# Token rows of a recurrent mixer: 128x128 transposes of two chunks and 64-partition evacuations in place of pairs of 64x64 products

## The chip, the cores and the metric

The kernel runs on one core of one Trainium2 chip. The time is the device time of one execution in microseconds (us). The core has TensorE (PE in the profile; its weight loads are PEld), VectorE (DVE), ScalarE (ACT), GpSimd (POOL) and SyncE (SP, which here only issues transfers). Products go to PSUM, in banks of 512 fp32 columns on 128 partitions; DVE and ACT bring them to SBUF ("evacuate" them).

## The reference

Two transformer blocks over 512 tokens of width 1024, the first with two layers. The second block's mixers are a delta-rule recurrence and a latent attention; a mixture of 32 experts follows. The recurrence has 8 heads of 64 channels:

```python
def step(state, inp):
    r_t, w_t, k_t, v_t, kk_t, a_t = inp
    sa = jnp.einsum('bhvk,bhk->bhv', state, -kk_t)
    state = (state * w_t[:, :, None, :]
             + sa[..., None] * (kk_t * a_t)[:, :, None, :]
             + v_t[..., None] * k_t[:, :, None, :])
    return state, jnp.einsum('bhvk,bhk->bhv', state, r_t)
...
_, ys = lax.scan(step, s0, xs)
```

A group norm per head, a bonus from r, k and v, and a gate follow; the result is multiplied by a branch matrix, gated, added to the latent attention's branch, and goes through an output projection to the router and the experts.

## The kernel before

The scan is done in 8 chunks of 64 tokens. Channels lie on partitions, two heads to a column tile of 128 (`ct`, 0 to 3), tokens along the free dimension. Four stages follow one another:

1. `prepare(pp, ct, hf)` (from L1352) makes the operands that need one chunk only, for one column tile and half of the chunks: 8 calls, here called prepare steps. It loads decays, k, a, r and v, takes a scan of the log decays (L1373), the normalised key `kk` (L1376 to L1385, with a mean over 64 channels by a product at L1380), a bonus (L1392 to L1396), exponentials `E1`, `E2` (L1399, L1402), and from these `KR` (L1404 to L1406), `bt` (in the tile `za`, L1409) and `kt` (in the tile `km`, L1411). Products within a chunk of `bt` and `kt` with `KR` give `SB` and `SK` (L1412 to L1417). Then come the token rows: `v`, `kt`, `kk` decayed and `bt` are turned so that tokens lie on partitions, for each head in its own half of the partitions (rows 0 to 63 the even head, 64 to 127 the odd one), into `KV`, `R` and `Btok` (L1432 to L1446). The even head is turned by a 64x64 transpose against the identity (L1438), the odd one by a product with a 64x64 identity that lies on partitions 64 to 127 (L1439, `id2`), since the result has to stay on the upper partitions. Three groups of products on these follow (L1447 to L1454; L1452 evacuates them).
2. `invert` (L1456) inverts triangular blocks of 32 on DVE, 31 steps of two instructions (L1463, L1465), for two column tiles at a time. Its input comes from `SB` over DRAM (L1421, L1426), and its result goes over DRAM (POOL's L1468, SP's L1474) into `TT`.
3. `solve` (L1478) starts from `TT` (a transpose on DVE at L1495, first products at L1501) and runs the chunk chain, for column tiles 0 and 1, then 2 and 3. The second inversion is issued among the steps of the first pair of solves.
4. Merge, output projection, router and experts (from L1667).

All products go through one helper: `products` (L1337 is the line that issues them). Dense products that need nothing of the recurrence (`merge_work`: the merge gates and the latent branch, recorded at L181 to L183) are kept for PE's gaps: `FREE = 54` pieces are issued behind the prepare steps, the others behind steps of the solves (`RATE = 0.5`). Their weights are split by ACT (L159) and DVE (L160) and their outputs evacuated at L1579, L1580 and L1592.

The code is recorded in program order; a scheduler then sets a fixed order on each engine. It takes instructions in program order where it can, and lets a later one go ahead where the earlier ones still wait. Each engine then works strictly through its order. PSUM has 8 banks: four for the tag "g" (dense products), two for "m" and two for "s"; the prepare steps' products take "m" by turns.

Of the kernel before, what the change touches and what calls it, by code (L numbers as in the profile page):

```python
# [26 lines left out]
RC = 64  # L27
# [8 lines left out]
def shape_constants():  # L36
# [10 lines left out]
    # rows: folded positions 0..127 (row 0 of the odd sines holds position 128, that of the even sines the cosine of  # L47
    # position 128); columns: even, odd frequencies
# [33 lines left out]
def build(tc, A, out):  # L82
# [45 lines left out]
    # ---- x in token rows  # L128
# [4 lines left out]
    def ln_and_exp(last):  # L133
        """The activation tables that serve logarithms and exponentials alike."""
        with tc.issue_after(last.ins):
            nc.scalar.preload_act_table_set("natural_log_exp_and_others")

    # ---- weight stream: raw rows -> two float32r parts whose sum is the weight
# [31 lines left out]
    def gemm_T_steps(chunks, Xk, evac, tiles=((0, 128), (128, 128))):  # L170
        """Weights stationary: psum [cols, tokens] for each of the column tiles (offset, width)."""
# [32 lines left out]
    def gemm_N(name, off, ld, K, cols, Xk, evac, kt=None, tags="gggg", between=None, ahead=True):  # L204
        """Tokens stationary: psum [tokens, cols] for each of the four token tiles."""
# [21 lines left out]
    def rsqrt_cols(pool, v, name):  # L227
        """1/sqrt of a few positive columns: an estimate from the exponent bits, then Newton steps."""
# [13 lines left out]
    def square_sums(pool, src, name, tag="sq", bufs=2):  # L242
        """Row sums of squares of the four token tiles."""
        ss = pool.tile([128, NT], F32, name=name + "_ss")
        for n in range(NT):
            sq = pool.tile([128, D], F32, tag=tag, name="sq", bufs=bufs)
            if n % 2:
                act(sq, src(n), AF.Square, accum_out=ss[:, n:n + 1])
            else:
                nc.vector.tensor_tensor_reduce(sq, src(n), src(n), 1.0, 0.0, OP.mult, OP.add, ss[:, n:n + 1])  # L250
        return ss

    def norm_rstd(pool, name, *ring):
        """Per token 1/rms of x, [128, 4]."""
# [10 lines left out]
    def transposed_split(w, Hh, Hl):  # L265
        """x times the norm weights, transposed and split: Hh, Hl lists of [128, 4, 512] tiles."""
# [8 lines left out]
    def along_tokens(r, dst):  # L275
        """Per token columns [128, 4] as rows of tokens on every partition."""
# [9 lines left out]
    # ---- rotary tables  # L286
# [24 lines left out]
    def rotary_tables(positions, freq, work):  # L311
        """Cosines, and sines with the first half of each pair of row halves negated."""
# [6 lines left out]
    def first_block_tables():  # L319
        # lower bounds of the decays: (direction, channel) rows, [layer, head]  # L320
# [78 lines left out]
    # ================= layers of the first block  # L399
    def mixers(l):  # L400
# [12 lines left out]
        # ---- projections and the recurrence  # L413
# [83 lines left out]
        def head(h, O):  # L497
# [8 lines left out]
            # carried state  # L506
# [30 lines left out]
            # pairs inside a chunk  # L537
# [87 lines left out]
        # ---- attention, Fourier mixing, output projection  # L625
# [11 lines left out]
        def fold(s, p):  # L637
            """Columns whose sums and differences the even and odd frequencies see: positions t and t + 256, then
            t and 256 - t."""
# [145 lines left out]
    def mlp_operands(l):  # L785
        """Of the moving operands of the up products' Winograd form (see mlp) the parts from two depth tiles, 2 k and
        2 k + 1. Of the tokens' halves the second comes first: B11, B22, B21, T1, T2, T3, -T4."""
# [24 lines left out]
    def mlp(l, operands):  # L812
        """Both products by Winograd's form of Strassen's seven. Up: of halves of the depth, of pairs of column tiles of
        the hidden layer, and of halves of the tokens. Down: of halves of the tokens (rows 2 are the first), of the
        pairs of column tiles of the hidden layer, and of halves of the columns."""
# [3 lines left out]
        with tc.tile_pool(name="mlp", bufs=1) as mp:  # L819
# [9 lines left out]
            class Spare:  # L829
                """Small tiles in the part of ar that is written last."""  # L830
# [9 lines left out]
            def up(g, c):  # L840
                """Yields once the two products of weights as they come are out."""
# [25 lines left out]
                def two(i, j):  # L867
                    """Two quarters of the result."""
# [54 lines left out]
            def product_steps(a, w, tag, parts):  # L923
                """Yields its sums before the last of the parts of a, and when done."""
# [100 lines left out]
    # ================= second block: its input is the normalised x, its mixers see that normalised again  # L1025
# [32 lines left out]
    # ---- columns of the recurrence, token shifted: low-rank parts kept, the others to DRAM  # L1058
# [6 lines left out]
    def rw_columns(pool, w_off, tiles, keep):  # L1065
        """Two column tiles of the recurrence's inputs; keep(s, z) takes them, token shifted."""
# [15 lines left out]
    def logistic(o, p, **kw):  # L1082
        """Logistic function of p plus twice the bias, by the hyperbolic tangent."""
# [3 lines left out]
    def low_rank(pool):  # L1087
        """Decays, rates and output gates, which depend on the low-rank inputs alone."""
# [30 lines left out]
    # ---- latent attention  # L1119
    def mla():  # L1120
# [6 lines left out]
        def rope(p, b, rows):  # L1127
            """Rows b to b+rows, pairs of 32 rows rotated together."""
# [65 lines left out]
        with tc.tile_pool(name="mla", bufs=1) as mp:  # L1194
            causal = mp.tile([128, T], F32, name="causal")
            nc.scalar.dma_start(causal, dram("causal", 0, [[T, 128], [1, T]]))
            # values of all heads, token rows, high and low parts side by side
# [24 lines left out]
            def up(pr):  # L1222
                """Queries and keys of two heads: rows 0-63 plain part, 64-127 rotary part."""
# [33 lines left out]
                # the rotary columns go to the upper rows; the lower rows of this product are not used  # L1257
# [55 lines left out]
    # ---- the branches' outputs, split  # L1313
# [4 lines left out]
    # ---- delta-rule recurrence  # L1318
    def rwkv():
        with tc.tile_pool(name="rw", bufs=1) as rp:  # L1320
# [12 lines left out]
            def products(n_, w_, p, l_, r_):  # L1333
                """Products of two heads for n_ chunks, w_ columns each."""
# [5 lines left out]
            # products without a place of their own: so many run ahead, the others at this rate behind the solves  # L1340
# [4 lines left out]
            # chunk-local parts and the blocks to invert come first where the outputs go  # L1345
# [6 lines left out]
            def prepare(pp, ct, hf):  # L1352
                """Chunk-local operands of two heads, for half of the chunks."""
# [20 lines left out]
                # normalised key direction  # L1374
# [15 lines left out]
                # bonus  # L1390
# [6 lines left out]
                # decayed operands  # L1397
# [6 lines left out]
                KR = pp.tile([128, 4, 2, 64], F32, tag="KR", name="KR", bufs=2)  # L1404
                tt(KR[:, :, 0], c4(kk), E1[:, :, 0:RC], OP.mult)
                tt(KR[:, :, 1], c4(r), E1[:, :, 1:], OP.mult)  # L1406
                nc.gpsimd.dma_start(rtd[ct, :, cs], KR[:, :, 1])
# [5 lines left out]
                for src, dst in ((bt, SB), (kt, SK)):  # L1413
                    p = ps("m")
                    products(4, 128, p, lambda c: src[:, c], lambda c: KR[:, c].rearrange("p a t -> p (a t)"))
# [12 lines left out]
                # token rows  # L1428
# [4 lines left out]
                for pair, dst in (((c4(v), kt), KV), ((KR[:, :, 0], bt), None)):  # L1433
                    p = ps("m")
                    for i, src in enumerate(pair):
                        for c in range(4):
                            o = p[:, (4 * i + c) * 64:(4 * i + c + 1) * 64]
                            nc.tensor.transpose(o[0:64], src[0:64, c], ident[0:64, 0:64])  # L1438
                            mm(o[64:], src[64:, c], id2[64:], start=True, stop=True)  # L1439
                    pv = p.rearrange("p (i c t) -> p i c t", i=2, c=4)  # L1440
                    if dst is not None:
                        act(dst, pv, AF.Copy)
                    else:
                        act(R[:, :, 0], pv[:, 0], AF.Copy)
                        act(Btok, pv[:, 1], AF.Copy)
                    yield  # L1446
# [726 lines left out]
```

## Time and profile before

| | us |
|---|---|
| median of 3 runs (2543.27 to 2547.39) | 2544.54 |
| span of the profiled execution | 2541.9 |
| around the span (median less span) | 2.6 |
| PE busy (share of the span) | 2239.0 (88%) |
| DVE busy | 2100.1 (83%) |
| ACT busy | 1290.7 (51%) |
| POOL busy | 1050.7 (41%) |
| mean granted clock of TensorE | 0.940 |

The page shows one profiled execution. Busy shares are means over stages with different limits, so the stage in which the change lies is read by itself: the prepare steps run from about 1800 to 1968 us of the span, the solves from 1995 to 2082, and the experts from about 2200 on. The clock is given as a share of 2.4 GHz: 1.00 is that level, 0.50 the level of 1.2 GHz, and a value between them is a mean over time. A row of a matmul gives how long one took from its start to its modelled end; matmuls overlap, so the time that one holds PE is read from the distance between starts.

### The profile page before, as it was taken

Reading aid. Unit: us, or ns where it says so; the run is one execution under the profiler, and the core shown is the slowest. Engines: PE = TensorE matmul, PEld = TensorE weight load, DVE = VectorE, ACT = ScalarE, POOL = GpSimd, SP = SyncE. Lnnn points to the kernel's source line nnn. Section 1 sums busy time; section 2 is a strip of 40 time slices with the busy share of each in tenths; the row PEclk is TensorE's granted clock in tenths of the full one; section 3 lists DMA queues with packets and bytes.
Section 4 is the critical chain, followed back from the end, with each engine's and each line's share of the span. In section 5 each row is a group of like instructions: output and inputs, shape, how many; then the busy total and the mean of one; then the engine's idle time right before and its main releaser. Section 6 shows DMA issues by size and latency. Waiting matters only on the chain. (4 is left out here: it accounts for less than half of the span.)

```text
span 2541.9 us, 34783 instructions
## 1 busy us (share of the span) xinstructions
PE 2239.0 (88%) x12842; PEld 1766.5 (69%) x12842; DVE 2100.1 (83%) x2988; ACT 1290.7 (51%) x1969; POOL 1050.7 (41%) x737
## 2 busy tenths in 40 slices
PE   7788997888789888898788888999999999699996
PEld 6666686768577776677577686667777777477764
DVE  6898889999998798899999999667635755799997
ACT  4355753343344444654343434565533232588984
POOL 1444336766763344326867665131112003222214
PEclk9999998999899999899899999999977999899998
DMA  5112031322222212123223220333432458599994
GB/s 150 50 50 93 19 123 42 107 76 83 75 59 87 59 51 75 48 52 119 75 59 108 75 84 25 118 111 108 138 77 78 126 197 300 201 327 320 322 339 153
DMA packets 215969, 302.37 MB, mean 119 GB/s; under 512 B 45719, under 2 KB 134167, under 8 KB 215792
## 3 DMA queue, kind: packets, MB, share of 16 engines
q1 hardware_dynamic: 179728, 262.57, 32.3%
q0 software_dynamic: 15680, 30.30, 3.5%
q10 hardware_dynamic: 20384, 7.21, 1.1%
q8 instruction: 103, 1.69, 0.3%
q14 instruction: 74, 0.61, 0.1%
HBM read 277.61 MB, written 40.14 MB: 125 GB/s over the span
## 5 line engine op out<-in xcount | busy, mean ns | idle before, releaser
L2025 DVE TENSOR_TENSOR wlo<-eraw,whi 128x1024 fp32r<-128x1024 f32 x190 | 229.4, 1233 | 32.6 <-ACT whi L2024 29.7
L937 DVE TENSOR_TENSOR wlo<-draw,whi 128x1024 fp32r<-128x1024 f32 x112 | 243.4, 2179 | 0.0
L865 PE MATMUL ps_g<-bh,wlo 128*128 128x256 f32 x640 | 187.4, 294 | 29.6 <-DVE wlo L353 21.9
L2024 ACT ACTIVATE whi<-eraw 128x1024 fp32r<-128x1024 f32 x190 | 197.1, 1070 | 30.1 <-PE ps_s L1950 23.4
L159 ACT ACTIVATE whi<-wraw 128x1024 fp32r<-128x1024 f32 x107 | 112.6, 1055 | 176.7 <-PE ps_g L182 107.1
L916 POOL TENSOR_TENSOR draw<-draw 128x1024 f32<-128x1024 f32 x64 | 175.5, 2757 | 47.1 <-DVE wlo L937 37.3
L863 PE MATMUL ps_g<-bh,whi 128*128 128x256 f32 x640 | 186.3, 291 | 1.6 <-ACT whi L352 1.1
L864 PE MATMUL ps_g<-bl,whi 128*128 128x256 f32 x640 | 185.7, 290 | 0.8 <-DVE bl L353 0.8
L936 ACT ACTIVATE whi<-draw 128x1024 fp32r<-128x1024 f32 x112 | 117.2, 1053 | 113.1 <-PE ps_g L943 76.2
L160 DVE TENSOR_TENSOR wlo<-wraw,whi 128x1024 fp32r<-128x1024 f32 x107 | 135.0, 1264 | 38.8 <-ACT whi L159 38.1
L865 PEld LDWEIGHTS ps_g<-bh,wlo 128*128 128x128 f32 x640 | 127.4, 200 | 33.4 <-DVE wlo L353 24.1
L353 DVE TENSOR_TENSOR wlo<-wraw,whi 128x512 fp32r<-128x512 f32 x96 | 127.1, 1345 | 24.0 <-ACT whi L352 23.9
L863 PEld LDWEIGHTS ps_g<-bh,whi 128*128 128x128 f32 x640 | 128.2, 200 | 2.5 <-ACT whi L352 1.3
L864 PEld LDWEIGHTS ps_g<-bl,whi 128*128 128x128 f32 x640 | 128.1, 200 | 1.3 <-DVE bl L353 1.0
L879 POOL TENSOR_TENSOR sums<-wraw 128x512 f32<-128x512 f32 x32 | 61.0, 1908 | 154.3 <-DMA wraw<-in_w_up_dram 69.0
L556 POOL TENSOR_TENSOR KE<-Dm,kk 128x512 f32<-128x512 f32 x56 | 78.3, 1411 | 108.9 <-ACT Dm L554 63.5
L181 PE MATMUL ps_g<-h2h,whi 128*128 128x512 f32 (+1 forms) x288 | 121.7, 423 | 0.0
L183 PE MATMUL ps_g<-h2h,wlo 128*128 128x512 f32 (+1 forms) x288 | 120.2, 418 | 0.0
L182 PE MATMUL ps_g<-h2l,whi 128*128 128x512 f32 (+1 forms) x288 | 120.1, 417 | 0.0
L181 PE MATMUL ps_g<-hhh,whi 128*128 128x512 f32 x288 | 115.5, 402 | 2.2 <-ACT whi L163 1.9
L183 PE MATMUL ps_g<-hhh,wlo 128*128 128x512 f32 x288 | 116.4, 404 | 0.4 <-DVE wlo L164 0.4
L182 PE MATMUL ps_g<-hhl,whi 128*128 128x512 f32 x288 | 115.0, 399 | 0.0
(811 smaller groups left out, 7344.2 us busy)
## 6 DMA issues: line engine op xcount, KB each, us to landing
eraw<-in_moe_w_gu_dram SPq DMA_DIRECT2D x61, 1024.0 KB, 17.7
wraw<-in_w_in_dram SPq DMA_DIRECT2D x74, 512.0 KB, 3.7
wraw<-in_w_up_dram SPq DMA_DIRECT2D x64, 512.0 KB, 4.5
draw<-in_w_down_dram SPq DMA_DIRECT2D x32, 1024.0 KB, 5.7
eraw<-in_moe_w_down_dram SPq DMA_DIRECT2D x30, 1024.0 KB, 17.9
wraw<-in_w_out_dram SPq DMA_DIRECT2D x24, 512.0 KB, 4.1
x<-in_x_dram SPq DMA_DIRECT2D x8, 512.0 KB, 4.9
wraw<-in_w_in_dram SPq DMA_DIRECT2D x16, 256.0 KB, 3.4
```

What stands on the lines that cost most here:

```text
L160: tt(lv, rv, f32(hv), OP.subtract)
L181: mm(o, hi[:, j, cs], xh, start=(k == 0), stop=False)
L182: mm(o, hi[:, j, cs], xl, start=False, stop=False)
L183: mm(o, lo[:, j, cs], xh, start=False, stop=(k == K - 1))
L353: tt(dl, src, f32(dh), OP.subtract)
L863: mm(o, hi[:, k], bh, start=(k == 0), stop=False)
L864: mm(o, hi[:, k], bl, start=False, stop=False)
L865: mm(o, lo[:, k], bh, start=False, stop=(k == 3))
L916: pt(o[:, hs], a[:, hs], b[:, hs], OP.subtract)
L937: tt(lo, rv, f32(hi), OP.subtract)
L2024: act(hi, rv, AF.Copy)
L2025: tt(lo, rv, f32(hi), OP.subtract)
```

## The change

`KR` is laid out by kind first (decayed keys, decayed r) and chunk second, so that two neighbouring chunks of one kind lie side by side. For the token rows, two neighbouring chunks of both heads, 128x128, are turned by one transpose: its output has (chunk of the two, token) on partitions and (head, channel) along columns. Where a chunk's and a head's half agree, ACT copies 64 partitions (two pairs of chunks, 64 columns each) to its place; where they differ, DVE copies them to the other half of the partitions. So each of the two PSUM banks of a step has four copies by each of the two engines, instead of one or two evacuations by ACT alone.

```diff
-                KR = pp.tile([128, 4, 2, 64], F32, tag="KR", name="KR", bufs=2)
-                tt(KR[:, :, 0], c4(kk), E1[:, :, 0:RC], OP.mult)
-                tt(KR[:, :, 1], c4(r), E1[:, :, 1:], OP.mult)
-                nc.gpsimd.dma_start(rtd[ct, :, cs], KR[:, :, 1])
+                KR = pp.tile([128, 2, 4, 64], F32, tag="KR", name="KR", bufs=2)
+                tt(KR[:, 0], c4(kk), E1[:, :, 0:RC], OP.mult)
+                tt(KR[:, 1], c4(r), E1[:, :, 1:], OP.mult)
+                nc.gpsimd.dma_start(rtd[ct, :, cs], KR[:, 1])
...
-                    products(4, 128, p, lambda c: src[:, c], lambda c: KR[:, c].rearrange("p a t -> p (a t)"))
+                    products(4, 128, p, lambda c: src[:, c], lambda c: KR[:, :, c])
...
-                for pair, dst in (((c4(v), kt), KV), ((KR[:, :, 0], bt), None)):
+                for pair, dst in (((c4(v), kt), (KV[:, 0], KV[:, 1])), ((KR[:, 0], bt), (R[:, :, 0], Btok))):
                     p = ps("m")
                     for i, src in enumerate(pair):
-                        for c in range(4):
-                            o = p[:, (4 * i + c) * 64:(4 * i + c + 1) * 64]
-                            nc.tensor.transpose(o[0:64], src[0:64, c], ident[0:64, 0:64])
-                            mm(o[64:], src[64:, c], id2[64:], start=True, stop=True)
-                    pv = p.rearrange("p (i c t) -> p i c t", i=2, c=4)
-                    if dst is not None:
-                        act(dst, pv, AF.Copy)
-                    else:
-                        act(R[:, :, 0], pv[:, 0], AF.Copy)
-                        act(Btok, pv[:, 1], AF.Copy)
+                        for b in range(2):
+                            transpose(p[:, (2 * i + b) * 128:(2 * i + b + 1) * 128], src[:, 2 * b:2 * b + 2])
+                    pv = p.rearrange("p (i b h t) -> p i b h t", i=2, b=2, h=2)
+                    for i in range(2):
+                        o = dst[i].rearrange("p (b c) t -> p b c t", c=2)
+                        for c in range(2):
+                            for h in range(2):
+                                src = pv[halves[c], i, :, h]
+                                if c == h:
+                                    act(o[halves[h], :, c], src, AF.Copy)
+                                else:
+                                    nc.vector.tensor_copy(o[halves[h], :, c], src)
                     yield
```

`transpose` is the helper at L126, which turns a 128x128 block against the full identity. Lines behind these are 4 higher in the changed kernel (the inversion's L1463 and L1465 are L1467 and L1469 there, the solve's L1495 is L1499); the copies are L1447 (ACT) and L1449 (DVE).

PE's order before, in the first prepare step, from the products with `KR` to the token rows of the tiles `zv` (v), `KR` (keys), `km` (kt) and `za` (bt); each group has four of each kind:

```order
L1337 MATMUL ps_m<-KR,km 64x128 x8
L1380 MATMUL ps_s<-sq,mean_69 128x256
L1438 MATMUL ps_m<-ident,zv 64x64
L1439 MATMUL ps_m<-id_9617,zv 64x64
...
L182 MATMUL ps_g<-h2l_12753,whi 128x512
L1438 MATMUL ps_m<-ident,KR 64x64
L1439 MATMUL ps_m<-id_9617,KR 64x64
...
L1438 MATMUL ps_m<-ident,km 64x64
L1439 MATMUL ps_m<-id_9617,km 64x64
```

The same place in the changed kernel:

```order
L1337 MATMUL ps_m<-KR,km 64x128 x8
L1380 MATMUL ps_s<-sq,mean_69 128x256
L126 MATMUL ps_m<-ident,zv 128x128 x2
L182 MATMUL ps_g<-h2l_12753,whi 128x512
L183 MATMUL ps_g<-h2h_12751,wlo 128x512
L126 MATMUL ps_m<-ident,KR 128x128 x2
L126 MATMUL ps_m<-ident,km 128x128 x2
L181 MATMUL ps_g<-h2h_12751,whi 128x512
L126 MATMUL ps_m<-ident,za 128x128 x2
```

Where 32 small instructions stood, eight stand, with dense products between them.

ACT's order before, at the first step's evacuations, with the engines that each row waits for:

```order
L1376 ACTIVATE sq<-zk,k_k 128x256 [waits DMAHW3_49]
L1442 ACTIVATE KV<-ps_m 128x512 [waits PE_49]
L1444 ACTIVATE R_14742<-ps_m 128x4x64 [waits PE_49]
L1445 ACTIVATE Btok_14743<-ps_m 128x256
L1382 ACT_TABLE_LOAD
L1382 ACTIVATE sq<-sq 128x256 [waits DVE_49]
L1452 ACTIVATE y0a<-ps_m 128x256 [waits PE_49]
```

ACT's order there in the changed kernel:

```order
L1376 ACTIVATE sq<-zk,k_k 128x256 [waits DMAHW3_49]
L1447 ACTIVATE KV<-ps_m 64x2x64 [waits PE_49]
L1382 ACT_TABLE_LOAD
L1382 ACTIVATE sq<-sq 128x256 [waits DVE_49]
L1447 ACTIVATE KV<-ps_m 64x2x64 [waits DVE_49]
L1447 ACTIVATE KV<-ps_m 64x2x64
L1447 ACTIVATE R_14742<-ps_m 64x2x64 [waits PE_49]
L1383 ACT_TABLE_LOAD
L1383 ACTIVATE sq<-sq 128x256 [waits Activation_49]
L1447 ACTIVATE KV<-ps_m 64x2x64 [waits DVE_49]
L1447 ACTIVATE R_14742<-ps_m 64x2x64 [waits DVE_49]
L1447 ACTIVATE Btok_14743<-ps_m 64x2x64
```

DVE's order there in the changed kernel (before, no instruction on DVE evacuates token rows):

```order
L1381 TENSOR_SCALAR sq<-ps_s 128x256 [waits PE_49]
L1449 COPY KV<-ps_m 64x2x64 [waits Activation_49]
L1449 COPY KV<-ps_m 64x2x64
L1449 COPY KV<-ps_m 64x2x64 [waits Activation_49]
L1449 COPY KV<-ps_m 64x2x64
L1449 COPY R_14742<-ps_m 64x2x64 [waits Activation_49]
L1449 COPY R_14742<-ps_m 64x2x64
L1385 SCALAR_TENSOR_TENSOR kk<-zk,k_k,sq 128x256 [waits DMAHW3_49,Activation_49]
L1387 TENSOR_SCALAR km<-za,k_a 128x256 [waits DMAHW4_49]
L1449 COPY Btok_14743<-ps_m 64x2x64 [waits Activation_49]
```

What moved: the evacuations stand on both engines, and one engine's copies of a bank wait for the other's.

DVE's order before, from the end of the first inversion (L1465 64x31) to the transpose with which the solve starts (L1495):

```order
L1465 TENSOR_TENSOR inverses<-inverses,outer 64x30x2
L1463 TENSOR_TENSOR outer<-inverses,blocks 64x31
L1465 TENSOR_TENSOR inverses<-inverses,outer 64x31
...
L1463 TENSOR_TENSOR outer<-inverses,blocks 64x207
L1465 TENSOR_TENSOR inverses<-inverses,outer 64x9x23
L1495 STREAM_TRANSPOSE T_16436<-TT_14782 128x256
L1463 TENSOR_TENSOR outer<-inverses,blocks 64x220
```

The same place in the changed kernel:

```order
L1469 TENSOR_TENSOR inverses<-inverses,outer 64x31
L1449 COPY R_14757<-ps_m 64x2x64 x2
L1449 COPY KV<-ps_m 64x2x64 x2
L1596 SCALAR_TENSOR_TENSOR gate<-gate,ps_g 128x512
L1449 COPY Btok_14758<-ps_m 64x2x64 x2
L1596 SCALAR_TENSOR_TENSOR gate<-gate,ps_g 128x512
L160 TENSOR_TENSOR wlo<-wraw,whi 128x1024 x3
L1499 STREAM_TRANSPOSE T_16348<-TT_14782 128x256
L1499 STREAM_TRANSPOSE T_16379<-TT_14784 128x256
L1583 TENSOR_TENSOR gate<-ps_g,Rb_12754 128x512 x2
L1467 TENSOR_TENSOR outer<-inverses,blocks 64x31
```

Before, nine of the second inversion's 31 steps stood ahead of the first transpose of the solve; now all of them stand behind both.

## Rows read from the trace of the kernel before

**Rows 1.** The page, busy tenths and granted clock in 40 equal slices:

```profile
PE   7788997888789888898788888999999999699996
...
PEclk9999998999899999899899999999977999899998
```

**Rows 2.** Windows; columns: us, PE, PEld, DVE, ACT, POOL busy, clock, DMA, GB/s:

```profile
1811.00:1979.00 168.00, 166.79 (x1245) 119.37 (x1245) 84.75 (x214) 61.24 (x116) 29.66 (x49) 0.80 0.34 96
1811.00:1914.00 103.00, 101.79 (x804) 71.84 (x803) 48.17 (x113) 42.15 (x80) 19.06 (x33) 0.80 0.37 101
1914.00:1979.00 65.00, 65.00 (x443) 47.53 (x442) 36.59 (x102) 19.09 (x36) 10.61 (x16) 0.79 0.28 88
1995.00:2038.00 43.00, 42.97 (x646) 32.90 (x644) 32.06 (x75) 12.86 (x26) 2.03 (x4) 1.00 0.33 88
1678.00:1790.00 112.00, 107.57 (x532) 84.24 (x530) 87.92 (x218) 68.78 (x153) 22.95 (x31) 1.00 0.27 84
```

**Rows 3.** Waits from 1811 to 1979: us in total, times, longest:

```profile
ACT KV L1442 <- PE ps_m L1439: 50.2, 8, 10.3
DVE dec L1403 <- ACT E L1399: 27.2, 5, 7.4
...
ACT R L1444 <- PE ps_m L1439: 18.5, 8, 3.1
```

**Rows 4.** Timeline of DVE, POOL, SP, PE after the inversion: start, duration, instruction:

```profile
1978.77 0.20 DVE L1465 TENSOR_TENSOR inverses<-inverses,outer 64x31 f32<-64x31 f32 x1
...
1979.26 0.56 POOL L1468 DMA_DIRECT2D xbd<-inverses  x1 [13.81 <-DVE outer L1463]
...
1982.72 3.86 SPq L1474 DMA_DIRECT2D TT<-xbd  x8
...
1995.32 0.69 PE L1501 MATMUL ps_s<-T,SB 32*32 32x32 f32 x32
```

**Rows 5.** Timeline of PE among the pairs, in two places:

```profile
1838.25 0.24 PE L1438 MATMUL ps_m<-ident,zv 64*64 64x64 f32 x1
...
1838.68 0.24 PE L1438 MATMUL ps_m<-ident,zv 64*64 64x64 f32 x1
...
1824.87 0.31 PE L1438 MATMUL ps_m<-ident,za 64*64 64x64 f32 x1
...
1825.51 0.31 PE L1438 MATMUL ps_m<-ident,za 64*64 64x64 f32 x1
```

**Rows 6.** Windows of 4 us in the first two prepare steps:

```profile
1824.00:1828.00 4.00, 4.00 (x26) 2.53 (x28) 0.00 (x0) 1.98 (x4) 0.00 (x0) 0.50 0.12 37
...
1836.00:1840.00 4.00, 4.00 (x46) 3.05 (x46) 3.97 (x10) 3.15 (x5) 2.11 (x3) 1.00 0.42 132
```

**Rows 7.** Timeline of PE: 128x128 transposes in the attention, dense products:

```profile
1692.30 0.52 PE L126 MATMUL ps_m<-ident,sb 128*128 128x128 f32 x3
...
1692.90 0.63 PE L126 MATMUL ps_m<-ident,sb 128*128 128x128 f32 x4
...
1645.75 0.40 PE L183 MATMUL ps_g<-h2h,wlo 128*128 128x512 f32 x1
...
1645.98 0.40 PE L181 MATMUL ps_g<-h2h,whi 128*128 128x512 f32 x1
```

**Rows 8.** Single lines (ns min/median/max, first to last start), then groups (busy, mean ns):

```profile
L1442 ACT ACTIVATE KV<-ps_m x8: 597/597/597, 1823.7 to 1957.2; 128x512 f32<-128x512 f32 x8
...
L1504 ACT ACTIVATE T<-ps_s x4: 374/376/377, 1996.1 to 2042.0; 32x256 f32<-32x256 f32 x4
...
L1395 DVE SCALAR_TENSOR_TENSOR bon<-ps_s,zv x8: 417/424/427, 1813.9 to 1943.9; 128x256 f32<-128x256 f32 x8
...
L1542 DVE TENSOR_TENSOR M<-ps_m,Psi x12: 210/214/215, 2018.7 to 2071.9; 128x64 f32<-128x64 f32 x12
...
L136 ACT ACT_TABLE_LOAD x6 | 7.7, 1283 | 0.1
...
L159 ACT ACTIVATE whi<-wraw 128x1024 fp32r<-128x1024 f32 x7 | 7.4, 1056 | 9.0 <-PE ps_g L182 9.0
```

## The prediction

> **What bounds the kernel now.** I read the page's busy slices first. In slices 30 and 31 of the 40 (1843 to 1970 us), where the second block's recurrence is prepared, PE is at 9 tenths or more while the granted clock falls to 7 tenths [rows 1]. Then the windows: from 1811 us, where the first prepare step gets going, to 1979 us, where the first inversion ends, PE is busy for 166.79 of 168 us at a mean clock of 0.80, DVE for 84.75 and ACT for 61.24 [rows 2]. PE is the limit there. The waits say the same from the other side: ACT stood 50.2 and 18.5 us in front of the evacuations of the token rows, waiting for the last of the small products, and DVE stood 27.2 us for an exponential that was queued behind those on ACT [rows 3]. So a microsecond taken from PE here is at first a whole one.
>
> What hangs on this stretch is the inversion for the first two column tiles, which DVE ends at 1978.97. Its result goes through DRAM (POOL's store at 1979.26, eight loads from 1982.72 on), and the first product of the solve starts at 1995.32, 16.3 us after the inversion [rows 4]. The solves, the merge, the routing and the experts follow one from the other. I take it that an earlier solve moves all of them by as much.
>
> **The pairs that go.** Each of the 8 prepare steps has 16 pairs of a 64x64 transpose and a 64x64 product: 128 pairs. Where the granted clock is 1.00, a pair follows the next by 0.43 us (1838.25 to 1838.68), where it is 0.50 by 0.64 us (1824.87 to 1825.51) [rows 5, 6]. So they hold PE for 55 to 82 us. A mean clock of 0.80 is 40% of the time at the lower level: 128 x (0.6 x 0.43 + 0.4 x 0.64) = 66 us.
>
> **The transposes that come.** 64 of 128x128. Four of that form in a row take 0.63 us, three 0.52 [rows 7], so each further one costs 0.11 us: 64 x 0.11 = 7 us; one alone takes 0.52 - 2 x 0.11 = 0.30, so if none overlapped 19 us. PE's net relief is 66 - 7 = 59 us, 36 to 75 by the ends.
>
> **The clock.** 40% of 168 us is 67 us at the 1.2 GHz level. It falls in the run of small pairs that begins at 1818 (0.50 from 1824 to 1828) and is back at 1.00 when the next run begins [rows 6]. The pairs take 0.4 x 128 x 0.64 = 33 of those 67 us; the other 34 would shrink by at most half, 17 us, if the level stayed up, and by nothing if it fell as before. I take 10, of which 6 before the inversion. In the attention stretch, 1678 to 1790, PE runs 128x128 transposes between dense products at a granted clock of 1.00 throughout [rows 2]; the new mix looks like that one. The Trainium skill ("TensorE: Matmul & The Clock Gate", Part 4: PE-mode transpose) says that transposes don't count for the clock as other work does; by that rule the 10 us are nothing, and the gain is 6 us smaller. The row of the attention stretch, where dense products stand between the transposes, does not show such a loss.
>
> **The evacuations.** Gone from ACT: 8 of 512 elements at 0.597 and 16 of 256 at about 0.38, 10.9 us [rows 8]. Added: 64 on ACT and 64 on DVE, each of 128 elements on 64 partitions. An evacuation's duration goes by the elements per partition: one of 32 partitions and 256 elements takes 0.376 [rows 8]. Between 256 and 512 elements ACT's grows by 0.22, so 128 cost 0.27: 64 x 0.27 = 17.3, net +6.4 us. On DVE 64 elements out of PSUM take 0.214 and 256 take 0.424 [rows 8]: 0.28 for 128, less if it overlaps its neighbour, so 64 x 0.20 to 0.28 = 13 to 18 us. DVE then has 98 to 103 us of work where it had 84.75. Crossing from one half of the partitions to the other is not shown apart on DVE: nothing to one more operation of 64 elements each (64 x 0.214 = 14 us). I take nothing, by ACT's row, which leaves partitions out and costs the same.
>
> **The handoffs.** In the changed order ACT's copies wait for DVE's and DVE's for ACT's, since they read one PSUM bank. Per step two banks pass between the engines four times each. DVE's normalised key stands behind such copies, and ACT's exponentials between them. A handoff costs nothing where the other engine is ahead, and up to a table load (1.283) and a weight part (1.056) [rows 8] where it stands behind these: 0 to 2.3 us, eight times a step. I take 1.5 us per step before the inversion, 8 in all, since the order puts other work between the copies of most steps. [...]
>
> **The sum.** Part one, to the start of the inversion at 1914: 103 us, PE busy 101.79 [rows 2]. Some 89 of the 128 pairs stand in it: -46 us, +5 for their transposes, -6 for the clock. The new order pulls some 50 more dense products forward into PE's gaps (176 stand ahead of that point in it, 127 ran before 1914 in the trace), at 0.23 us (1645.75 to 1645.98) [rows 7]: +11. 103 - 46 + 5 - 6 + 11 = 67, with the handoffs 75: the inversion starts at 1886. Part two, the inversion among the last prepare steps: 65 us, with DVE busy for 36.59 [rows 2]. There DVE becomes the limit: 36.6 + 24 copies x 0.25 = 42.6, and 7 of stalls: 50. It ends at 1936 against 1979, 43 us earlier. The way through DRAM stays (16 us; the 54 dense products left for it take 12). The second inversion, of which the first steps ran before the solve's transposes until now, starts behind them in the new order; DVE is busy for 32.06 of the 43 us in which it has to be done [rows 2], and I put 3 us on that. Gain 43 - 3 = 40 us.
>
> The profiled execution has a span of 2541.9 and the median of the runs is 2544.54, so 2.6 us lie around it. 2541.9 - 40 + 2.6 = 2504.5, told as 2504.
>
> What is left I put at nothing: KR is laid out by kind and then by chunk, so that a product reads its 128 columns in two runs, and the store of KR to DRAM has longer runs, on POOL, which POOL's idle time hides. If two runs cost as much as a product's second pass (128 products, 0.11 us each), it is 14 us on PE, inside the range.
>
> **Rivals.**
> *The handoffs set the pace.* ACT has 61.24 + 6.4 us and, in the new order, seven more table loads (9 us), so 77 us in order, with DVE waiting at each exchange. At 2.3 us on two of a step's eight handoffs it is 8 x 4.6 = 37 us instead of the 15 (8 + 7) that I took: gain 18, and at two and a half 9. Time 2518 to 2536. For it: neither engine may pass its waiting copy. Against: DVE has the inversion's steps to put between. 20 in 100.
> *PE's relief counts in full.* DVE's 100 us without gaps in place of 168: 68 us less, 2477; 2490 at half of the way. It needs the two queues to mesh. 10 in 100.
> *The solve starts no earlier.* If the inversion's inputs, which POOL stores and loads again, or the loads of a step came last, PE would idle for what it gains. Against: the long waits before are for products and for ACT, none for a load [rows 3]. Within 0.2% (5 us) of 2544.5: 4 in 100.
> *Slower.* The split evacuations, with a table load ahead of them, lengthen a prepare step from its present 19.1 us ((1957.2 - 1823.7)/7 by ACT's evacuations [rows 8]). DVE's work per step is 100/8 = 12.5 us, so it needs 6.6 us of stall, nearly three handoffs per step at full price. At four (9.2 us) a step takes 21.7 and the kernel 8 x 2.6 = 21 us more, 2565. 5 in 100.
>
> **How the numbers follow.** The forecast has 61 in 100; its own range is 2490 to 2520, from PE's relief at its ends and the handoffs from nothing to twice what I took. With part of the first two rivals the range for 8 in 10 is 2484 to 2532. Faster by over 0.2%, which is about what a measurement of this kernel can tell from no change: 0.91; within it 0.04; slower 0.05.
>
> **What would show it.** PE no longer busy throughout between the first prepare step and the first solve product, and its clock near 1.00 in the first part; ACT's two waits for the small products gone; in their place waits of DVE for ACT's copies and the reverse, of 1 to 2 us per step; the inversion ending near 1936 and the first solve product 12 to 17 us behind it; the experts' stretch as long as now, and some 40 us earlier. If the waits between the copies add up to over 35 us, the first rival holds; if the clock is still 0.80, that term was wrong; if the inversion is earlier and the experts are not, the step from the solve on was.

## The result, and the profile after

The changed kernel takes 2506.18 us (median of four runs, 2496.02 to 2508.82), the kernel before 2545.71 in the runs beside it: a ratio of 0.983 with a 95% interval of 0.981 to 0.985, or 39.5 us less. The profiled execution has a span of 2505.7 us (before 2541.9). The first prepare step's key (L1385) stands at 1810.4 us in the trace before and at 1814.9 after; in the kernels run here, which share all code up to that point, it lies between 1808.7 and 1822.2. The stages are therefore counted from that key (us, from the timelines):

| from the first key to | before | after | earlier by |
|---|---|---|---|
| start of the first inversion | 103.9 | 67.9 | 36.0 |
| end of the first inversion | 168.6 | 111.1 | 57.5 |
| first product of solve (0, 1) | 184.9 | 129.3 | 55.6 |
| first product of solve (2, 3) | 227.6 | 183.5 | 44.0 |
| first product of the experts | 379.9 | 338.7 | 41.2 |

In a second trace of the changed kernel (after_again, below) the five stand at 67.7, 110.8, 129.0, 183.5 and 334.1: the first four agree within 0.4 us, the last by 4.6, so a few us behind the solves are not told apart here.

From about L1440 on, a line of the kernel before has a number greater by 4 in the changed one (the inversion's L1463 and L1465 are L1467 and L1469). The page of the changed kernel, busy tenths and granted clock in 40 slices, answers to [rows 1]:

```profile
PE   7798997888788888997887888999998899699995
...
PEclk9999998899999999899998999999998999799998
```

The two slices with a clock of 7 tenths at 1843 to 1970 us [rows 1] are gone: slice 30 (1817 to 1879) has 9, slice 31 has 8. PE, at 9 there before, is at 8 tenths in slices 31 and 32. The windows, with the columns of [rows 2], give from the top: first key to inversion, the inversion, its way through DRAM, the solve of tiles (0, 1) up to the first product of (2, 3):

```profile
1815.00:1883.00 68.00, 64.80 (x569) 50.69 (x569) 57.72 (x148) 52.94 (x106) 16.71 (x32) 1.00 0.57 162
1883.00:1926.00 43.00, 36.21 (x333) 27.59 (x331) 40.09 (x124) 22.70 (x51) 8.78 (x14) 0.84 0.22 69
1926.00:1944.00 18.00, 16.39 (x104) 13.06 (x104) 9.50 (x20) 3.98 (x11) 5.41 (x9) 0.91 0.84 232
1944.20:1998.50 54.30, 45.01 (x647) 33.70 (x646) 47.84 (x106) 18.63 (x33) 2.76 (x5) 0.98 0.34 96
```

The first stretch has a granted clock of 1.00, the 2.4 GHz level, from end to end, where it was 0.80. In the second DVE is the limit (40.09 of 43 us). In the fourth DVE is busy for 47.84 of 54.30 us and PE stands idle for 9.3 us; before, the same work took 42.7 us with PE full [rows 2].

The waits from 1815 to 1926 us (in total, times, longest) answer to [rows 3]:

```profile
ACT KV L1447 <- PE ps_m L126: 16.8, 6, 4.7
...
ACT KV L1447 <- DVE KV L1449: 5.8, 8, 1.4
PE ps_m L1337 <- ACT KV L1447: 5.4, 6, 2.0
DVE KV L1449 <- ACT KV L1447: 4.6, 4, 1.7
```

ACT's 50.2 and 18.5 us before the small products have become 16.8. The new waits between the two engines' copies are 5.8 and 4.6 us, with 1.7 and 0.5 more of ACT for `Btok` and `R`: 12.6 us, 1.6 per prepare step. PE, which had no such wait before, stands 5.4 us in front of products that read the copies. The copies themselves, min/median/max in ns:

```profile
L1447 ACT ACTIVATE KV<-ps_m x32: 253/272/275, 1824.2 to 1927.3; 64x128 f32<-64x128 f32 x32
L1449 DVE COPY KV<-ps_m x32: 283/288/295, 1824.5 to 1927.0; 64x128 f32<-64x128 f32 x32
L126 PE MATMUL ps_m<-ident,zv x16: 271/273/421, 1822.9 to 1923.6; 128*128 128x128 f32 x16
```

All of DVE's copies cross from one half of the partitions to the other, none of ACT's does. The timeline after the inversion answers to [rows 4]:

```profile
1926.31 0.57 POOL L1472 DMA_DIRECT2D xbd<-inverses  x1 [3.70 <-DVE inverses L1469]
...
1929.34 4.00 SPq L1478 DMA_DIRECT2D TT<-xbd  x8
...
1934.84 0.45 DVE L1499 STREAM_TRANSPOSE T<-TT 128x256 f32<-128x256 f32 x1 [1.10 <-DMA TT<-xbd]
1941.77 1.39 DVE L1583 TENSOR_TENSOR gate<-ps_g,Rb 128x512 f32<-128x512 f32 x2 [6.48 <-PE ps_g L183]
1943.19 0.19 DVE L1467 TENSOR_TENSOR outer<-inverses,blocks 64x31 f32<-64x31 f32 x1
...
1944.19 0.69 PE L1505 MATMUL ps_s<-T,SB 32*32 32x32 f32 x32
```

The transposed blocks are there at 1935.3, but PE still has dense products up to 1944, and DVE's queue holds a gate evacuation that waits 6.48 us for them, with the second inversion behind it. Before, that inversion had begun at once behind the first one, 16.1 us ahead of the solve (its first write at 1979.2); now it is 0.8 us ahead (1943.4). Behind the second inversion the way to the solve of tiles (2, 3) shows up too:

```profile
1987.12 0.21 DVE L1469 TENSOR_TENSOR inverses<-inverses,outer 64x31 f32<-64x31 f32 x1
...
1990.58 4.04 SPq L1478 DMA_DIRECT2D TT<-xbd  x8
...
1997.98 0.44 DVE L1499 STREAM_TRANSPOSE T<-TT 128x256 f32<-128x256 f32 x1
...
1998.48 0.75 PE L1505 MATMUL ps_s<-T,SB 32*32 32x32 f32 x20 [6.56 <-DVE T L1499]
```

The fourth stretch, cut at the end of that inversion:

```profile
1944.20:1987.30 43.10, 40.70 (x634) 31.80 (x634) 38.85 (x91) 11.84 (x23) 1.08 (x2) 1.00 0.30 89
1987.30:1998.50 11.20, 4.31 (x15) 1.91 (x13) 8.98 (x16) 6.79 (x10) 1.68 (x3) 0.89 0.51 124
```

For 43.1 us DVE works at the second inversion with other instructions between its steps. Then its result takes 11.2 us through DRAM and DVE's queue to the first product, and 6.9 of PE's 9.3 idle us lie there. Before, the second inversion ended at 2017.4, 20.6 us ahead of that product, and this way was hidden.

### The profile page after: what moved, and what is told of

Read it like the earlier page. It is cut to its first block, busy times and chain, and to the rows that moved or that the text cites. A ratio compares the mean times of both kernels' runs of the same rounds, so it can differ in the third digit from the quotient of the medians.

```text
span 2505.7 us, 34249 instructions
## 1 busy us (share of the span) xinstructions
PE 2184.8 (87%) x12522; PEld 1735.1 (69%) x12522; DVE 2119.6 (85%) x3052; ACT 1306.5 (52%) x2016; POOL 1047.9 (42%) x737
## 5 line engine op out<-in xcount | busy, mean ns | idle before, releaser
L879 POOL TENSOR_TENSOR sums<-wraw 128x512 f32<-128x512 f32 x32 | 58.9, 1840 | 154.9 <-DMA wraw<-in_w_up_dram 75.5
## 6 DMA issues: line engine op xcount, KB each, us to landing
eraw<-in_moe_w_down_dram SPq DMA_DIRECT2D x30, 1024.0 KB, 18.5
```

## The experiments

All times below are medians beside runs of the kernel before on the same chip (2547.5 to 2549.2); the ratio is to that kernel, with its 95% interval.

**The layout of `KR` alone.** The kernel before with this edit, pairs and wide evacuations left as they were:

```diff
-KR = pp.tile([128, 4, 2, 64], F32, tag="KR", ...)     # chunk, kind
+KR = pp.tile([128, 2, 4, 64], F32, tag="KR", ...)     # kind, chunk
-products(4, 128, p, lambda c: src[:, c], lambda c: KR[:, c].rearrange("p a t -> p (a t)"))
+products(4, 128, p, lambda c: src[:, c], lambda c: KR[:, :, c])
```

> The kernel before with one part of the change alone: KR by kind and then by chunk; the 64x64 pairs and ACT's wide evacuations stay. Theory (the gain is PE's time for the pairs): nothing moves, 2540 to 2551 us, the first inversion ends within 3 us of 1979. Rival (the layout does part of it, by the longer runs of the store of KR to DRAM): faster by 5 us or more. Rival (a product that reads its 128 columns in two runs costs a second pass of 0.11 us): 128 products, 14 us slower, and the products of KR take over 0.30 us instead of 0.269.

2545.61 us, 0.9995 (0.998 to 1.0011). From its key to the end of the first inversion it takes 169.5 us (168.6 before). The products that read two runs, in ns, and under them those of the kernel before:

```profile
L1337 PE MATMUL ps_m<-KR,za x128: 269/269/320, 1819.3 to 1951.5; 64*64 64x128 f32 x128
L1337 PE MATMUL ps_m<-KR,za x128: 269/269/321, 1815.8 to 1947.0; 64*64 64x128 f32 x128
```

The median of 269 is the same. The layout gives and costs nothing that can be told.

**Each transpose nine times.**

```diff
-transpose(p[:, (2 * i + b) * 128:(2 * i + b + 1) * 128], src[:, 2 * b:2 * b + 2])
+for _ in range(9):
+    transpose(p[:, (2 * i + b) * 128:(2 * i + b + 1) * 128], src[:, 2 * b:2 * b + 2])
```

> The changed kernel with each of the 64 transposes of 128x128 issued nine times into the same place of PSUM: same data, same evacuations, same handoffs, and about as much PE time as the pairs had (eight more at 0.11 us each, 64 x 0.88 = 56 us). Theory (PE's time is what the change took away): most of the gain goes again; the first inversion ends between 1955 and 1980 and the kernel takes 2530 to 2555 us; the granted clock stays near 1.00 in the first part, since no small products stand there. Rival (the form of the evacuations, not PE's time, gave the gain): 2506 +- 8 us. Rival (transposes let the clock fall, by the rule of the Trainium skill, TensorE: Matmul & The Clock Gate, Part 4): the clock is at 0.50 in the runs of transposes, each takes about 0.22 us, and the kernel takes over 2565 us.

2536.76 us, 0.9951 (0.9933 to 0.9968): most of the gain is gone. Timeline of PE in one prepare step, and two windows, the second from the first key to the first product of the solve:

```profile
1841.56 2.13 PE L126 MATMUL ps_m<-ident,km 128*128 128x128 f32 x18
1843.52 2.13 PE L126 MATMUL ps_m<-ident,KR 128*128 128x128 f32 x18
```

```profile
1840.00:1847.00 7.00, 7.00 (x66) 7.00 (x65) 4.03 (x13) 1.09 (x4) 3.78 (x7) 1.00 0.54 129
...
1817.00:1989.00 172.00, 166.93 (x1512) 142.88 (x1510) 132.79 (x350) 75.12 (x162) 31.42 (x55) 1.00 0.40 113
```

18 transposes take 1.96 us, 0.109 each, so 512 more are 56 us of PE. The solve begins 172.2 us behind the first key, against 129.3 with single transposes and 184.9 before: of the 55.6 us won there, the added transposes take 42.9 back. The other 12.7 us are put down to the clock, which is 1.00 here all the way to the solve and was 0.80 in the prepare steps before [rows 2], with 576 transposes (63 us) in the place of pairs that would take 55 us at 1.00. That is argued: the split evacuations stay in this kernel too, and no run tells their share from the clock's. From 1840 to 1847 us PE does nothing but transposes, and the clock stays at 1.00: the rival by the rule of the Trainium skill ("TensorE: Matmul & The Clock Gate", Part 4: PE-mode transpose) does not hold here. One expectation failed: the first inversion ends 106 us behind the key, 5 us earlier than in the changed kernel, since in the new order 49 dense products stand ahead of its end instead of 213, and the last prepare step (its key at 1926.7) behind it; the time is lost between there and the solve. So the two kernels compare at the solve, ahead of which both have about as many dense products (264 and 269), and not at the inversion.

**Half of the change.** Values and keys by the new way, `R` and `Btok` by the pairs and ACT's wide evacuations:

```diff
+if dst[1] is Btok:
+    ...  # 64x64 pairs, act(dst[i], pv[:, i], AF.Copy), as before
+    continue
```

> Half of the change: the values and the keys by 128x128 transposes and split copies, R and Btok by the 64x64 pairs and ACT's wide evacuations as before (KR in the new layout). Theory (PE's time for the pairs and the granted clock that falls in their runs are the gain): half of the pairs, 27 to 41 us, stay on PE, so about half of the gain: 2515 to 2535 us, with the clock between 0.80 and 0.94 over the prepare steps. Rival (the gain comes from one of the two banks, or needs both): within 8 us of the one or the other kernel.

2520.36 us, 0.9881 (0.985 to 0.9913). The window from its first key to its first inversion's end, with PE full again:

```profile
1814.60:1957.20 142.60, 140.77 (x1091) 101.40 (x1091) 92.90 (x246) 65.63 (x140) 27.30 (x48) 0.84 0.38 110
```

The first inversion ends 142.9 us behind the key, between the 168.6 before and the 111.1 after, and the solve starts at 158.3, 26.6 of the 55.6 us earlier; the clock of 0.84 lies between 0.80 and the 0.94 of the whole change's two stretches. One bank's pairs give about half, so those of the other bank make up the rest.

**The copies dealt by bank.** The first bank's eight copies all on DVE, the second's all on ACT (j numbers the banks):

```diff
-if c == h:
+if j:
     act(o[halves[h], :, c], src, AF.Copy)
```

With it ran the changed kernel itself once more (after_again) and the two that follow.

> The changed kernel once more, as the measure for the three kernels beside it on the same chip: 2496 to 2509 us.

> The changed kernel with the copies dealt by bank instead of by half: of each prepare step the eight copies out of the first bank (values and keys) all on DVE, the eight out of the second (R and Btok) all on ACT. Work per engine is the same, and no bank passes between the engines. Seven table loads of ACT go as well (30 in the recurrence instead of 37), 9 us of ACT's time. Theory (the handoffs cost what their waits add up to, 5.8 + 4.6 + 1.7 us, but PE is busy for 64.8 of the 68 us of the first part and DVE for 40.1 of the 43 of the second, so that little of it can come back): 0 to 6 us faster than the changed kernel, the inversion ending between 1920 and 1926. Rival (the handoffs and the table loads set the pace): 10 to 20 us faster. Rival (eight copies in a row on one engine, 2.2 us, hold up the products behind them): 5 us or more slower than the changed kernel.

The changed kernel took 2504.55 us (0.9832, 0.9813 to 0.9851), the one dealt by bank 2498.69 (0.9816, 0.9798 to 0.9834). 5.9 us lie between the medians, while the intervals overlap: a gain of the small size expected, not proven by itself. The trace shows no wait between the two engines' copies any more, and PE's idle time in the first stretch as it was (60.53 of 63.80 us busy, against 64.80 of 68):

```profile
1812.80:1876.60 63.80, 60.53 (x591) 47.43 (x590) 56.92 (x149) 47.57 (x105) 16.68 (x32) 1.00 0.57 160
1876.60:1918.80 42.20, 33.37 (x298) 25.93 (x298) 39.11 (x124) 19.18 (x47) 9.19 (x15) 0.92 0.25 76
```

Its first inversion ends 106.2 us behind the key instead of 111.1, but its solve starts at 129.4, no earlier than the changed kernel's 129.3. What is gained shows at the second inversion, which now starts 9.3 us ahead of the solve instead of 0.8: the solve of (2, 3) starts at 176.8 instead of 183.5. Each engine's copies now cross to the other half in half of the cases, and take what they took:

```profile
L1447 ACT ACTIVATE R<-ps_m x32: 250/272/275, 1822.5 to 1917.0; 64x128 f32<-64x128 f32 x32
```

```profile
L1449 DVE COPY KV<-ps_m x64: 274/288/296, 1822.0 to 1919.3; 64x128 f32<-64x128 f32 x64
```

So 12.6 us of waits between copies, together with seven table loads, were worth about 5 us at the first inversion and, in all, 6 to 7 at the second solve. No run parts the waits from the table loads.

**Fewer dense products ahead of the solve.** FREE, the number of groups of six dense products issued ahead of the solves, from 54 to 48, and to 44:

```diff
-FREE, RATE = 54, 0.5
+FREE, RATE = 48, 0.5
```

> The changed kernel with 48 instead of 54 groups of dense products (6 products each) issued ahead of the solves; the other six groups go among the solves. DVE's gate evacuation, behind which the second inversion stood from 1935 to 1943, then stands behind the inversion's first steps in DVE's order, and PE is free for the solve some 8 us earlier. Theory (the second inversion's late start is what cost 11.6 us between the solves of the first two and of the last two tiles): the second inversion starts 6 to 9 us earlier, and the kernel is 4 to 9 us faster than the changed kernel, 2496 to 2502. Rival (PE has no room for the six groups among the solves): within 3 us of the changed kernel. Rival (the solves' chain, not the second inversion, sets the pace there): the same as the changed kernel, with a solve of the last two tiles that starts no earlier.

> As the one with 48 groups, but with 44 ahead of the solves: 60 products, 14 us of PE, moved behind. Theory: the second inversion starts no earlier than with 48, since its inputs and the solve's transposes come no earlier, PE stands idle for some 5 us before the solve, and the kernel is 0 to 5 us slower than with 48. Rival (the fewer dense products ahead the better): 3 us or more faster than with 48.

2524.22 us (0.9906, 0.9881 to 0.9931) and 2528.86 (0.992, 0.9899 to 0.9941): 20 and 24 us slower than the changed kernel. What was expected of 48 groups was wrong; with 44 the median is 4.6 us above that of 48, as expected, but the intervals overlap. With 48 the second inversion did start at 1929.0, 8 us earlier from the key, but among its steps on DVE stands the low part of a weight, which waits for its high part on ACT, and that is queued behind the solve's evacuations. The timeline of DVE with 48 groups:

```profile
1931.65 0.30 DVE L1467 TENSOR_TENSOR outer<-inverses,blocks 64x135 f32<-64x135 f32 x1
1944.51 1.23 DVE L160 TENSOR_TENSOR wlo<-wraw,whi 128x1024 fp32r<-128x1024 f32 x1 [12.56 <-ACT whi L159]
1945.76 0.30 DVE L1469 TENSOR_TENSOR inverses<-inverses,outer 64x135 f32<-64x135 f32 x1
```

The wait was moved, not removed, and the last of the products put behind now stand in front of the merge, from 2039 to 2048.5 us.

**More of them ahead.** 60 groups in the changed kernel, then 60 and 66 with the copies dealt by bank:

> The changed kernel with 60 instead of 54 groups of dense products ahead of the solves (36 more products, 8.4 us of PE). With 48 groups the kernel had lost 20 us, 12.6 of them where a weight part on DVE stood among the second inversion's steps and waited for ACT. Theory (the stretch of the second inversion is set by what DVE has to do in its order there, weight parts and evacuations of the dense products among the inversion's steps; PE has 8 us of idle time ahead, between 1905 and 1925, that more groups could fill): 0 to 8 us faster than the changed kernel, 2496 to 2505, with less DVE work beside the second inversion. Rival (PE: the solve starts 8 us later and nothing is made up): 2510 to 2515.

> The copies dealt by bank and 60 groups together. Theory (two separate places, the prepare steps and the second inversion): the two gains add up, 6 us by the bank and what the 60 groups alone give, 2490 to 2500 us. Rival (both fill the same idle time of PE): no faster than the better of the two alone.

> As the one before, with 66 groups. Theory: PE's idle time ahead of the solve is used up, so the solve starts 8 us later than with 60, and PE idles beside the second inversion: 2 to 8 us slower than with 60. Rival (the fewer dense products stand beside the second inversion the better): 3 us or more faster than with 60.

2491.95 us (0.9789, 0.9769 to 0.9809), 2493.8 (0.9794, 0.9778 to 0.9809) and 2487.13 (0.9761, 0.9744 to 0.9778). The first is 4 us below what was expected; the gains of bank and groups don't add up, as the rival of the second run said; the third was expected slower and is faster. From the first product of solve (0, 1) to that of (2, 3), with 60 groups, and in the next fence with 66 by bank:

```profile
1958.50:2004.70 46.20, 44.57 (x645) 34.03 (x644) 36.28 (x84) 13.22 (x25) 1.63 (x3) 0.96 0.31 92
```

```profile
1959.40:2002.00 42.60, 42.60 (x645) 32.88 (x644) 28.41 (x65) 12.16 (x25) 2.03 (x4) 1.00 0.46 138
```

With 66 the stretch is back at its 42.7 us of before, and PE is full. What differs is the second inversion's head start over the solve (from its first write to the solve's first product) and with it DVE's work beside the solve:

| kernel | head start, us | stretch, us | DVE busy in it, us |
|---|---|---|---|
| changed, 54 | 0.8 | 54.3 | 47.84 |
| 60 | 6.8 | 46.2 | 36.28 |
| by bank, 54 | 9.3 | 47.3 | 40.03 |
| half of the change, 54 | 11.5 | 44.0 | 32.87 |
| before, 54 | 16.1 | 42.7 | 31.76 |
| by bank, 66 | 22.2 | 42.6 | 28.41 |

The solve itself starts 16 us later than in the changed kernel (145.2 us behind the key); the stretch gives 11.7 back, and the way from solve (2, 3) to the experts takes 132.4 instead of 155.1 (150.7 in after_again): 72 dense products, 16.7 us, no longer stand there.

**The control, and all of them ahead.** The kernel before with 66 groups, and the copies by bank with all 80:

> The kernel before with 66 instead of 54 groups of dense products ahead of the solves: the control for the runs with more groups. Theory (the groups pay only since the changed kernel leaves PE idle ahead of the solves and DVE full beside them; in the kernel before PE is busy throughout in both stretches): 0 to 5 us off the kernel before, 2542 to 2552. Rival (54 was a poor number for either kernel): 10 to 18 us faster than the kernel before, and then those runs say nothing about the change.

> The copies dealt by bank and all 80 groups of dense products ahead of the solves. Theory (with 66 groups the solves already run without idle time on PE by their own products and the 14 left; with none left PE waits for the solves' chain): 3 to 12 us slower than with 66, 2490 to 2500. Rival (the fewer beside the solves the better, as from 48 to 66): 2477 to 2485.

The control takes 2544.39 us, 0.9988 (0.9974 to 1.0003): no difference that can be told. Its solve starts 17.7 us later from the key, and the way from solve (2, 3) to the experts is 21.4 us shorter. In its trace, from the first key to the first inversion's end, PE has no idle time for the products to fill:

```profile
1814.00:1980.00 166.00, 165.98 (x1239) 118.79 (x1238) 81.87 (x205) 59.01 (x112) 29.22 (x48) 0.78 0.34 94
```

With all 80 ahead it is 2484.2 us, 0.975 (0.9728 to 0.9771), expected slower than with 66 and not told apart from it. These two versions beat both kernels, at 0.975 and 0.976 of the kernel before where the change alone is at 0.983; 66 groups pay with the change and not without it, where PE has no idle time. The kernel before was not run with 80.

## Why the prediction was right

*The pairs on PE.* Right in kind and nearly in size. From the key to the inversion PE's busy time fell from 101.79 to 64.80 us, although 70 more dense products of 0.23 us (16 us) stand in it, 154 instead of 84: a relief of 53 us, where 46 - 5 + 6 = 47 had been set. (Of more dense products, 50 had been set.) Nine transposes in the place of one take 42.9 of the 55.6 us back, and with half of the pairs left the inversion ends 25.7 us earlier and not 57.5.

*The clock.* 10 us were taken, within 0 to 17. With as much PE time put back in large transposes, the solve starts 12.7 us earlier than before. If all of that is the clock's, it lies inside the range and above the value; no run shows the clock alone. The Trainium skill ("TensorE: Matmul & The Clock Gate", Part 4: PE-mode transpose), weighed in the prediction, speaks against it, and the trace disagrees: 1.00 over 7 us of transposes alone.

*The copies.* ACT 0.272 against an estimated 0.27, DVE 0.288 against 0.28.

*The handoffs* were the term too large in cost. The waits came out as forecast, 1.6 us per step against 1.5, but the sum charged all 8 and 7 us to the path. In the first stretch PE was idle for 3.2 us in all, in the second DVE for 2.9. So part one took 67.9 us, not 75, and part two 43.2, not 50: the inversion ended 57.5 us earlier from the key, not 43.

*The second inversion's place* was the term too small: 3 us set, 11.6 measured (54.3 against 42.7). The prediction looked at DVE's 32.06 us of work in the 43 of the stretch before [rows 2], and not at the part of the inversion that had been done ahead of it. With its head start gone, that part comes on top, and the way of its result through DRAM, 20.6 us of cover before, comes to stand on the path: 43.1 + 11.2 us. The runs with 60 and 66 groups give the head start back, and the stretch shrinks to 46.2 and 42.6 us, but they also move DVE's splits and evacuations for the dense products. Two runs keep the 54 groups: by bank and with half of the change, head starts of 9.3 and 11.5 us go with stretches of 47.3 and 44.0. So the head start counts at an unchanged number of groups. The moved work seems to count too, since 60 groups take less (46.2) with a smaller head start (6.8); how much is each one's share stays open.

*The way through DRAM* was kept at 16 us and took 18.2, just outside the 12 to 17 named. DRAM was not what it lasted for: the transposed blocks were there 9.3 us behind the inversion, and PE's dense products took the rest; with 44 groups the solve starts 8.3 us behind the inversion. The way from solve (2, 3) to the experts was 155.1 and, in after_again, 150.7 against 152.3: as long as before, as forecast. PE goes idle in the last prepare steps and again ahead of the second solve, and the clock falls with it:

```profile
1904.90:1924.90 20.00, 13.91 (x112) 10.78 (x110) 17.83 (x57) 7.79 (x19) 1.96 (x3) 0.66 0.10 27
1984.90:2004.90 20.00, 12.51 (x123) 8.03 (x124) 13.78 (x27) 8.53 (x14) 1.68 (x3) 0.78 0.60 177
```

Both are stretches of the changed kernel in which PE waits (13.91 and 12.51 us busy of 20); the clock was 0.66 and 0.78.

So the forecast of 40 us met the 39.5 with two terms that missed in opposite directions: 14.5 us too little at the inversion, some 13 too little loss behind it. That they cancel to half a us is luck; that PE's time and not the handoffs decided is not. *The handoffs set the pace* is refuted as a rival: its own mark was 35 us of waits, there were 12.6, and without any handoff (and without the seven table loads) the median is about 6 us lower.

## What to carry to other kernels

Work taken from a busy engine counts in full only as far as the next engine is idle; price a wait by what the limiting engine loses in that stretch, not by its own length. When a stage is made faster, look at what used to run in the shadow of its end: here a second inversion had 16 us of head start before the solve, lost it, and with it some 12 us, until the filler products were dealt out anew. A number tuned for the old balance (54 groups) is worth trying again, with the same number on the kernel before as control.

## What the runs showed of the hardware

Back-to-back transposes of 128x128 in float32 follow each other by 0.109 us and did not let the granted clock fall in 7 us of nothing else, while runs of 64x64 transposes and products at 0.43 us a pair did [rows 5, 6]. An evacuation of 64 partitions and 128 elements costs the same whether it crosses to the other half of the partitions or not: on ACT 0.272 us where none and where half of them cross, on DVE 0.288 where all and where half of them do. And a product whose moving operand lies in two runs of 64 columns takes the same 0.269 us as one in a single run of 128.
